# Expert weights through fifteen 8 KB buffers instead of six of 16 KB in a hybrid decoder block

## The chip, the cores and the metric

The kernel runs on one core of a Trainium2 chip. The metric is the device time of one execution in microseconds (us), read as the median of several runs; lower is better. Engine names: PE is the tensor engine (PEld its weight loads), DVE the vector engine, ACT the scalar engine, POOL the general engine, SP the engine whose queue issues most transfers. Sizes of on-chip buffers are given per partition: a buffer of 16 KB holds 16 KB in each of the 128 partitions, 2 MB in all.

## What is computed

One decoder layer on 512 tokens of width 2048, all float32:

```python
xn = rmsnorm(h, norm_mix_w)
proj = xn @ w_in                       # queries, keys, values, gates of both branches
fox_o = forgetting_attention(...)      # 8 heads
ret_o = silu(rg) * groupnorm(retention(...))   # 8 heads
merged = sum(sigmoid(gate_logit + b_gate) * (branches @ w_branch))
h = h + merged @ w_out
hn = rmsnorm(h, norm_ffn_w)
# router: best group of 4, best 2 of its 8 experts (32 experts in all)
# per token and chosen expert e:  y = (silu(x @ w1[e]) * (x @ w3[e])) @ w2[e]
h = h + weighted sum of the two y
return rmsnorm(h, norm_final_w)
```

The weights of the 32 experts are 3 x 2048 x 512 floats each, 12 MB an expert and 384 MB together. Each is read once.

## The kernel before

**First stage, up to the router.** `units_a()` lists 118 blocks of dense weights of 1 MB, two of which lie next to each other in one row of `wA`. `Stream.unit` loads two blocks at once (2 MB, a run of 16 KB in each partition) into one of two buffers of the pool `raw`, and splits each block into a rounded high part (an ACT cast, L96) and a low part (a DVE subtraction, L97) in one of two 16 KB buffers of the pool `split`. PE multiplies with these. The last dense product is `w_out` (L593 to L595); the router's logits (L557, L558) come from the same tokens and close the stage.

**Expert stage.** Every expert has one block of at most 64 tokens (`SLOTS`). `prep_e(e)` gathers them: products of a selection matrix with the three bf16 parts of the hidden state (L720, PE), gathered into `xs`. `gemm1` (matmuls at L745 named `ab<-wraw,xs`) multiplies `xs` with `w1` and `w3`, `gemm2` (matmuls at L745 named `y<-wraw,gs`) the gated result with `w2`. The result is scattered into a DRAM buffer `ybuf`. A further loop for experts with more than 64 tokens is in the program and is not entered with this data.

The weights `wM` come in pieces of 2 MB: four for `gemm1`, two for `gemm2`. A `gemm1` piece holds in each partition a run of 8 KB of `w1` and one of `w3`; a `gemm2` piece is one run of 16 KB of `w2`:

```python
loads = iter(itertools.cycle([raw, raw, split, split, raw2, raw2]))
def piece_tile(pl):
    return pl.tile([P, 2, 2048], F32, name="wraw", tag="whl" if pl is split else "wraw")
...
        for i in range(2 if part else 4):
            w = piece_tile(next(loads))
            nc.sync.dma_start(w, (w2 if part else w13)(a["wM"][e], i))
```

So six buffers go round: the two of `raw`, the two of `split`, and two of a pool `raw2` that lies in memory which the first stage uses for other things. All loads are issued on SP in the order of the program: `gemm1` of experts 0 and 1, then `gemm2` of expert e-1 behind `gemm1` of expert e+1, and so on. A load waits until PE has read what its buffer held before, and until an earlier load that used the same of eight completion semaphores has landed. The order on PE is that of a scheduler, which interleaves `gemm2`, the next gather and the next `gemm1`.

**End.** `combine` runs over four groups of 128 tokens. It reads the two expert outputs of a token from `ybuf` (2 MB a group, into the same six buffers), and per quarter of the width adds residual, outputs and the last expert's share in PSUM on PE, then `res` on DVE (L942), squares on ACT (L947), normalizes (L949 to L959) and stores. `res` lies in a buffer of `raw2`. The last expert is not scattered: its rows `ys`, and the final norm's weight `fw`, lie in the pool `yout`.

Of the kernel before, what the change touches and what calls it, by code (L numbers as in the profile page):

```python
# [21 lines left out]
P = 128  # L22
D = 2048
# [9 lines left out]
MAXBLK = 15  # L33
EPS = 1e-6
# [23 lines left out]
class Stream:  # L58


    def __init__(self, tc, raw, split):
        self.tc, self.nc, self.raw, self.split = tc, tc.nc, raw, split
        self.src, self.cur, self.half = None, None, 2

    def first(self, src):

        self.cur, self.half = self.raw.tile([P, 2, 2048], F32, name="wraw"), 0
        self.src = src

    def unit(self, src_of=None, after=None, whole=False):  # L70
        nc = self.nc
        if self.half == 2:
            self.cur, self.half = self.raw.tile([P, 2, 2048], F32, name="wraw"), 0
            nc.sync.dma_start(self.cur, src_of())
        w = self.cur[:, self.half, :]
        if whole:
            self.half += 1
            return w, None
        hl = self.split.tile([P, 2, 2048], F32R, name="whl")
        hi, lo = hl[:, 0], hl[:, 1]  # L80
        n = 2048
        if after is not None:
            with self.tc.issue_after(after[0]), self.tc.issue_after(after[1]):
                nc.scalar.copy(hi, w)
                nc.vector.tensor_sub(lo, w, hi.bitcast(F32))
            self.half += 1
            return hi, lo
        if self.src is not None:
            n = 512 if self.half == 0 else 2048
        for q in range(2048 // n):  # L90
            c = slice(q * n, (q + 1) * n)
            if self.src is not None:
                nc.sync.dma_start(w[:, c], self.src[:, self.half, c])
                if n < 2048:
                    self.fill(q)
            nc.scalar.copy(hi[:, c], w[:, c])  # L96
            nc.vector.tensor_sub(lo[:, c], w[:, c], hi[:, c].bitcast(F32))  # L97
        self.half += 1
        if self.half == 2:
            self.src = None  # L100
        return hi, lo
# [25 lines left out]
def hybrid_block(ctx, tc, a, out):  # L127
# [12 lines left out]
    raw = hold("raw", 2)  # L140
    split = hold("split", 2)
# [4 lines left out]
    def unit(kind, i, g=0, after=None):  # L146
        assert order[pos[0]] == (kind, i, g), (order[pos[0]], kind, i, g)
        k = pos[0]
        pos[0] += 1
        if k == 0:  # L150
            stream.first(a["wA"][0].rearrange("p (u n) -> p u n", u=2))
        return stream.unit(lambda: a["wA"][k // 2].rearrange("p (u n) -> p u n", u=2), after)
# [52 lines left out]
    stream.fill = lambda q: load_x(0, q)  # L205

# [13 lines left out]
    def proj_T(kind, i):  # L220
        hi, lo = unit(kind, i)
        acc = pj.tile([P, T], F32, name="acc")
        for k in range(KT):
            wh, wl = hi[:, k * P:(k + 1) * P], lo[:, k * P:(k + 1) * P]
# [5 lines left out]
    def proj_V(kind, q):  # L230
        v = [vp.tile([P, T], F32, name="v") for _ in range(NT)]
        accs = [pj.tile([P, T], F32, name="acc") for _ in range(NT)]
        for g in range(4):
            if kind == "fv" and q == 0 and g:
                load_x(g)
            hi, lo = unit(kind, q, g)
            for t in range(NT):
                for kk in range(4):
                    k = 4 * g + kk
                    s = slice(t * P, (t + 1) * P)  # L240
                    wh, wl = hi[:, kk * T:(kk + 1) * T], lo[:, kk * T:(kk + 1) * T]
# [221 lines left out]
    with pool("mtmp", 2, reuse_waits="tile") as mt:  # L463
        for j in range(KT):
            hi, lo = unit("br", j, after=done[3] if j == 1 else None)
            gs, bs = [], []
            for n in range(2):
# [4 lines left out]
                for k in range(H):  # L472
                    i = n * H + k
                    wh, wl = hi[:, i * P:(i + 1) * P], lo[:, i * P:(i + 1) * P]
# [46 lines left out]
    with pool("wr", 1, reuse_waits="tile") as wrp, pool("ht", 2, reuse_waits="tile") as ht:  # L521
# [11 lines left out]
        for c in range(4):  # L533
# [49 lines left out]
            for g in range(4):  # L583
                hi, lo = unit("wo", c, g)
                for t in range(NT):
# [3 lines left out]
                    for kk in range(4):  # L589
                        k = 4 * g + kk  # L590
                        s = slice(t * P, (t + 1) * P)
                        wh, wl = hi[:, kk * T:(kk + 1) * T], lo[:, kk * T:(kk + 1) * T]
# [35 lines left out]
    fold = rp[0].tile([P, P], F32, name="fold")  # L628
    half = P // 2
    nc.vector.tensor_add(fold[:, :half], ident[:, :half], ident[:, half:])  # L630
# [137 lines left out]
    last_ins = []  # L768
    yp = []

    def gemm2(blk, pieces, late=False):

        gs, idx = blk
        if late:
# [300 lines left out]
```

## Time and profile before

| | us |
|---|---|
| median of 3 runs (2462.07 to 2462.34) | 2462.12 |
| the profiled execution, its own time | 2461.32 |
| its span in the trace | 2459.5 |
| PE busy in the span | 2355.6 |
| DVE busy | 737.6 |
| ACT busy | 488.6 |
| POOL busy | 233.4 |

Busy time of the engines is an average over stages with different limits. The slices and the windows (rows below) tell the stages apart: in each, the unit that is never idle sets the time. A transfer is cut into packets, one for each contiguous run; 16 DMA engines share them. The profile gives the bytes and the packets of a stretch, and the share of the 16 engines' time.

### The profile page before, as it was taken

Reading aid. Unit: us, or ns where it says so; the run is one execution under the profiler, and the core shown is the slowest. Engines: PE = TensorE matmul, PEld = TensorE weight load, DVE = VectorE, ACT = ScalarE, POOL = GpSimd, SP = SyncE. Lnnn points to the kernel's source line nnn. Section 1 sums busy time; section 2 is a strip of 40 time slices with the busy share of each in tenths; the row PEclk is TensorE's granted clock in tenths of the full one; section 3 lists DMA queues with packets and bytes.
Section 4 is the critical chain, followed back from the end, with each engine's and each line's share of the span. In section 5 each row is a group of like instructions: output and inputs, shape, how many; then the busy total and the mean of one; then the engine's idle time right before and its main releaser. Section 6 shows DMA issues by size and latency. Waiting matters only on the chain. (4 is left out here: it accounts for less than half of the span.)

```text
span 2459.5 us, 35971 instructions
## 1 busy us (share of the span) xinstructions
PE 2355.6 (96%) x16110; PEld 1605.8 (65%) x16114; DVE 737.6 (30%) x1271; ACT 488.6 (20%) x617; POOL 233.4 (9%) x328
## 2 busy tenths in 40 slices
PE   8999999999999999999999979999988999999986
PEld 6888888888888888888888854544444444444422
DVE  4444445544442222244433231111111111111105
ACT  5222223222222222232223310000010000000013
POOL 0000000100100000001003121111111111111002
PEclk9999999999999999999999989999999999999998
DMA  7233334232223333244432369999999999999996
GB/s 289 98 107 128 108 101 139 79 110 73 107 78 128 128 124 117 109 151 154 146 125 87 146 267 416 414 421 422 422 421 422 422 422 422 421 422 422 422 423 249
DMA packets 85839, 594.22 MB, mean 242 GB/s; under 512 B 7800, under 2 KB 24248, under 8 KB 34640
## 3 DMA queue, kind: packets, MB, share of 16 engines
q1 hardware_dynamic: 56704, 549.48, 55.1%
q0 software_dynamic: 7856, 25.61, 3.1%
q10 hardware_dynamic: 21120, 16.78, 2.1%
q8 instruction: 128, 2.10, 0.3%
q14 instruction: 31, 0.25, 0.0%
HBM read 562.72 MB, written 37.24 MB: 244 GB/s over the span
## 5 line engine op out<-in xcount | busy, mean ns | idle before, releaser
L745 PE MATMUL ab<-wraw,xs 128*64 128x512 f32 x2048 | 461.8, 603 | 39.2 <-DMA wraw<-in_wM_dram 39.0
L225 PE MATMUL acc<-xh,whl 128*128 128x512 f32 x1152 | 453.2, 393 | 0.0
L227 PE MATMUL acc<-xh,whl 128*128 128x512 f32 x1152 | 453.2, 393 | 0.0
L226 PE MATMUL acc<-xl,whl 128*128 128x512 f32 x1152 | 452.7, 393 | 0.0
L96 ACT CAST whl<-wraw 128x2048 fp32r<-128x2048 f32 (+1 forms) x122 | 228.0, 1869 | 780.3 <-PE acc L227 412.4
L745 PEld LDWEIGHTS ab<-wraw,xs 128*64 128x64 f32 x2048 | 144.0, 138 | 325.4 <-issue 252.0
L97 DVE TENSOR_TENSOR whl<-wraw,whl 128x2048 fp32r<-128x2048 f32 (+1 forms) x122 | 275.3, 2257 | 202.2 <-ACT whl L96 201.9
L226 PEld LDWEIGHTS acc<-xl,whl 128*128 128x128 f32 x1152 | 216.4, 188 | 46.4 <-issue 1.4
L225 PEld LDWEIGHTS acc<-xh,whl 128*128 128x128 f32 x1152 | 216.5, 188 | 45.8 <-issue 0.5
L227 PEld LDWEIGHTS acc<-xh,whl 128*128 128x128 f32 x1152 | 216.4, 188 | 45.8 <-issue 1.4
L745 PE MATMUL y<-wraw,gs 128*64 128x512 f32 x1024 | 235.0, 602 | 1.7 <-DMA wraw<-in_wM_dram 1.2
L720 PEld LDWEIGHTS <-h 128*128 128x128 bf16 x6144 | 189.9, 98 | 49.5 <-issue 49.1
L720 PE MATMUL gp<-S,h 128*128 128x64 bf16 x6144 | 199.2, 193 | 1.2 <-issue 1.2
L723 DVE TENSOR_TENSOR xs<-gp,nfw 128x512 f32<-128x512 f32 x64 | 41.9, 688 | 417.0 <-PE ab L745 375.2
L745 PEld LDWEIGHTS y<-wraw,gs 128*64 128x64 f32 x1024 | 69.4, 137 | 119.2 <-issue 114.1
L705 POOL TENSOR_SCALAR S<-slot,rank 128x128 bf16<-128x128 f32 x124 | 73.4, 602 | 705.3 <-PE gp L720 673.8
L758 ACT ACTIVATE ab<-ab,rs 128x512 f32<-128x512 f32 x32 | 22.0, 687 | 524.4 <-PE ab L745 506.7
L242 PE MATMUL acc<-whl,xh 128*128 128x512 f32 x256 | 101.8, 401 | 6.2 <-ACT xh L201 6.2
L795 ACT COPY ysb<-y 64x512 f32<-64x512 f32 x62 | 35.8, 579 | 339.0 <-PE y L745 330.6
L243 PE MATMUL acc<-whl,xh 128*128 128x512 f32 x256 | 102.6, 401 | 0.0
L593 PE MATMUL acc<-whl,mh 128*128 128x512 f32 x256 | 100.4, 392 | 0.0
L594 PE MATMUL acc<-whl,mh 128*128 128x512 f32 x256 | 100.2, 391 | 0.0
(302 smaller groups left out, 2121.6 us busy)
## 6 DMA issues: line engine op xcount, KB each, us to landing
wraw<-in_wM_dram SPq DMA_DIRECT2D x192, 2048.0 KB, 23.7
wraw<-in_wA_dram SPq DMA_DIRECT2D x59, 2048.0 KB, 7.8
ybuf<-zero ACTq DMA_DIRECT2D x8, 1024.0 KB, 5.7
gate<-gs ACTq DMA_DIRECT2D x32, 256.0 KB, 2.0
g<-gate POOLq DMA_DIRECT2D x32, 256.0 KB, 2.9
wraw<-ybuf SPq DMA_DIRECT2D x4, 2048.0 KB, 26.4
xt<-in_x_dram SPq DMA_DIRECT2D x4, 1024.0 KB, 6.4
hc<-in_x_dram POOLq DMA_DIRECT2D x4, 1024.0 KB, 5.5
```

The source lines that it names most:

```text
L96: nc.scalar.copy(hi[:, c], w[:, c])
L97: nc.vector.tensor_sub(lo[:, c], w[:, c], hi[:, c].bitcast(F32))
L225: nc.tensor.matmul(acc, wh, xh[:, k], start=(k == 0), stop=False)
L226: nc.tensor.matmul(acc, wh, xl[:, k], start=False, stop=False)
L227: nc.tensor.matmul(acc, wl, xh[:, k], start=False, stop=(k == KT - 1))
L242: nc.tensor.matmul(accs[t], xh[:, k, s], wh, start=(k == 0), stop=False)
L243: nc.tensor.matmul(accs[t], xh[:, k, s], wl, start=False, stop=False)
L593: nc.tensor.matmul(accs[t], mh[k][:, s], wh, start=(k == 0), stop=False)
L594: nc.tensor.matmul(accs[t], mh[k][:, s], wl, start=False, stop=False)
L705: i = eng.tensor_scalar(S[:, t], slot1.rearrange("p a b -> p (a b)"), rsel[:, t:t + 1], None, op0=OP.is_equal)
L720: nc.tensor.matmul(gp[:, d], h3[i][:, t, (8 * g + d) * P:(8 * g + d + 1) * P], S[:, t, :SLOTS], start=(t == 0 and i == 0), stop=(t == NT - ...
L745: nc.tensor.matmul(acc[m * SLOTS:(m + 1) * SLOTS], st, w[m], start=first, stop=last)
```

## The change

The buffers are halved in size and fifteen instead of six: `raw` four of 8 KB, `split` four of 8 KB, `raw2` seven of 8 KB. The first stage loads one block of 1 MB at a time, and splits it in two halves of 1024 columns. The expert weights move in pieces of 1 MB: eight for `gemm1`, four for `gemm2`. A piece holds two runs of 4 KB in each partition, for `w2` as well. The last expert's rows `ys` and the final norm's weight `fw` move out of `yout` into the buffers `r1` and `r0` of `raw2` while the last 24 loads go round in the other thirteen. `combine` loads 1 MB at a time and writes its result over the first expert output instead of into `res`. A small matrix `fold` is no longer made.

```diff
-    raw = hold("raw", 2)
-    split = hold("split", 2)
+    raw = hold("raw", 4)
+    split = hold("split", 4)
...
+    def parts(self, w, after=None, n=1024):
...
+        for m in range(2):
+            hl = self.split.tile([P, 2, 1024], F32R, name="whl")
+            wm = w[:, m * 1024:(m + 1) * 1024]
...
+                    nc.scalar.copy(hl[:, 0, c], wm[:, c])
+                    nc.vector.tensor_sub(hl[:, 1, c], wm[:, c], hl[:, 0, c].bitcast(F32))
...
-    raw2 = scC.enter_context(pool("raw2", 2, reuse_waits="tile"))
+    raw2 = scC.enter_context(pool("raw2", 1, reuse_waits="tile"))
+    slots = [(raw, "wraw")] * 4 + [(split, "whl")] * 4 + [(raw2, f"r{i}") for i in range(NR2)]
+    loads = itertools.cycle(slots)
+    kept = set()
+
+    def buffer(shape=(P, 2, 1024), dtype=F32, name="wraw", slot=None):
+
+        if slot is not None:
+            kept.add(slots[slot][1])
+        while slot is None:
+            pl, tag = next(loads)
+            if tag not in kept:
+                break
+        else:
+            pl, tag = slots[slot]
+        return pl.tile(list(shape), dtype, name=name, tag=tag)
...
-        for g in range(4):
+        for g in range(8):
             w = next(pieces)
-            for kk in range(4):
-                k = 4 * g + kk
+            for kk in range(2):
+                k = 2 * g + kk
...
         for q in range(2):
-            w = next(pieces)
             y = psY.tile([P, DE], F32, name="y")
             for k in range(4):
-                halves_mm(y, gs[:, k], [w[:, m, k * DE:(k + 1) * DE] for m in range(2)], k == 0, k == 3)
+                if k % 2 == 0:
+                    w = next(pieces)
+                halves_mm(y, gs[:, k], [w[:, m, k % 2 * DE:(k % 2 + 1) * DE] for m in range(2)], k == 0, k == 3)
...
-        return we.rearrange("(m q) p (u n) -> m q u p n", m=3, u=2)[:2, g // 2, g % 2].rearrange("m p n -> p m n")
-
-    def w2(we, q):
-        return we[4 + q].rearrange("p (u n) -> p u n", u=2)
-
-    def pieces_of(e, part):
-        for i in range(2 if part else 4):
-            w = piece_tile(next(loads))
-            nc.sync.dma_start(w, (w2 if part else w13)(a["wM"][e], i))
+        return we.rearrange("(m q) p (u n) -> m q u p n", m=3, n=1024)[:2, g // 4, g % 4].rearrange("m p n -> p m n")
+
+    def w2(we, g):
+        return we[4 + g // 2].rearrange("p (u v n) -> v p u n", u=2, v=2)[g % 2]
+
+    def pieces_of(we, part):
+        for i in range(4 if part else 8):
+            w = buffer()
+            nc.sync.dma_start(w, (w2 if part else w13)(we, i))
             yield w
...
-            yb = piece_tile(next(loads) if first else raw)
-            nc.sync.dma_start(yb, yv[t])
-            return [[yb[:, k, c * T:(c + 1) * T] for c in range(4)] for k in range(2)]
+            ys = [buffer((P, D)) for _ in range(2)]
+            for k in range(2):
+                nc.sync.dma_start(ys[k], yv[t][:, k])
+            return ys
...
-            y0, y1 = ybs[t] if first else load_y(t)
-            r = raw2.tile([P, D], F32, name="res", tag="wraw")
+            r, y1 = ybs[t] if first else load_y(t)
...
-                nc.vector.scalar_tensor_tensor(r[:, cs], y0[c], wtf[:, 0, t:t + 1], pr,
+                nc.vector.scalar_tensor_tensor(r[:, cs], r[:, cs], wtf[:, 0, t:t + 1], pr,
                                                op0=OP.mult, op1=OP.add)
```

The change moves instructions on two engines at places that matter below. On SP, at the passage from the dense weights to the expert weights, the queue held this before (the number behind `wraw` tells tiles apart; the brackets name the semaphores that a load waits for, `DMAHW` those of SP's own earlier transfers, `DMASW` those of POOL's):

```order
L817 DMA wraw_9384<-in_wM_dram 128x2x2048 [waits DMAHW2_49,DVE_49]
L817 DMA wraw_9394<-in_wM_dram 128x2x2048 [waits DMAHW3_49,DVE_49]
L817 DMA wraw_9404<-in_wM_dram 128x2x2048 [waits PE_49]
L817 DMA wraw_9414<-in_wM_dram 128x2x2048 [waits PE_49]
L817 DMA wraw_9649<-in_wM_dram 128x2x2048 [waits DMASW4_49,DMASW5_49,DMASW3_49,DMASW6_49,DMASW2_49,Pool_49]
L817 DMA wraw_9659<-in_wM_dram 128x2x2048 [waits DMASW4_49,DMASW5_49,DMASW3_49,DMASW6_49,DMASW2_49,DMASW7_49,DMASW1_49,DMASW0_49]
L817 DMA wraw_9669<-in_wM_dram 128x2x2048 [waits DMAHW4_49,PE_49]
L817 DMA wraw_9679<-in_wM_dram 128x2x2048 [waits DMAHW5_49,PE_49]
```

Of the changed kernel the same place, from the last load into `split` on:

```order
L826 DMA wraw_9900<-in_wM_dram 128x2x1024 [waits PE_49]
L826 DMA wraw_10131<-in_wM_dram 128x2x1024 [waits DMASW3_49,DMASW2_49,DMAHW7_49,DVE_49,PE_49]
L826 DMA wraw_10137<-in_wM_dram 128x2x1024 [waits DMASW5_49,DMAHW0_49,DMASW4_49,Pool_49]
L826 DMA wraw_10143<-in_wM_dram 128x2x1024 [waits DMAHW1_49,DMASW6_49,DMASW0_49]
L826 DMA wraw_10149<-in_wM_dram 128x2x1024 [waits DMAHW2_49]
L826 DMA wraw_10155<-in_wM_dram 128x2x1024 [waits DMASW5_49,DMASW6_49,DMASW4_49,DMASW7_49,DMASW3_49,DMAHW3_49,DMASW2_49,DMASW1_49]
L826 DMA wraw_10161<-in_wM_dram 128x2x1024 [waits DMAHW4_49]
L826 DMA wraw_10167<-in_wM_dram 128x2x1024 [waits DMAHW5_49]
L826 DMA wraw_10173<-in_wM_dram 128x2x1024 [waits DMAHW6_49,PE_49]
L826 DMA wraw_10405<-in_wM_dram 128x2x1024 [waits DMAHW7_49,PE_49]
```

Eight loads of 1 MB stand ahead of `wraw_10131`, the first into `raw2` (buffer `r0`), where it was four of 2 MB; this load now waits for PE and DVE too, because `r0` lies on a pool of the router's stage (its last reader is the logits matmul, L558 of before), and it heads a queue of seven loads into `raw2`.

On PE, when `gemm1` of expert 4 (tile `ab`) and `gemm2` of expert 2 (tile `y`) run, the order before was this (gathers between left out):

```order
L745 MATMUL y_10506<-wraw_10504,gs_9993 64x512 x8
...
L745 MATMUL y_10519<-wraw_10517,gs_9993 64x512 x8
...
L745 MATMUL ab_10533<-wraw_10534,xs_10302 64x512 x8
...
L745 MATMUL ab_10533<-wraw_10544,xs_10302 64x512 x8
...
L745 MATMUL ab_10533<-wraw_10554,xs_10302 64x512 x8
```

And it is this in the changed kernel:

```order
L758 MATMUL y_11018<-wraw_11019,gs_10495 64x512 x4
L758 MATMUL y_11018<-wraw_11025,gs_10495 64x512 x4
...
L758 MATMUL ab_11051<-wraw_11052,xs_10816 64x512 x4
...
L758 MATMUL ab_11051<-wraw_11082,xs_10816 64x512 x4
...
L758 MATMUL ab_11051<-wraw_11088,xs_10816 64x512 x4
...
L758 MATMUL y_11033<-wraw_11034,gs_10495 64x512 x4
L758 MATMUL y_11033<-wraw_11040,gs_10495 64x512 x4
...
L758 MATMUL ab_11051<-wraw_11094,xs_10816 64x512 x4
```

The loads are issued in the order of their numbers. Counted from 0, `wraw_11034` and `wraw_11040` are the loads 42 and 43, and `wraw_11052` to `wraw_11094` the loads 44 to 51: the second half of this `gemm2`, which stood ahead of the next `gemm1`, now stands behind seven of its eight pieces, and its two buffers stay taken as long.

## Rows read from the trace of the kernel before

**Rows 1.** The page: mean busy share of the DMA engines, 40 slices of the span.

```profile
DMA  7233334232223333244432369999999999999996
```

**Rows 2.** Windows: start:end, length, busy of PE, PEld, DVE, ACT, POOL; clock, DMA, GB/s.

```profile
0.00:1340.00 1340.00, 1333.17 (x6080) 1097.86 (x6081) 547.02 (x819) 357.19 (x381) 84.88 (x133) 1.00 0.34 123
1500.00:1600.00 100.00, 98.83 (x1296) 52.56 (x1293) 11.98 (x28) 6.69 (x12) 12.45 (x20) 1.00 1.00 415
2300.00:2400.00 100.00, 85.22 (x568) 33.06 (x565) 9.98 (x21) 10.47 (x19) 3.60 (x4) 0.98 1.01 422
2420.00:2460.00 40.00, 21.00 (x64) 9.35 (x65) 29.06 (x77) 15.72 (x39) 10.50 (x8) 0.78 0.38 153
```

**Rows 3.** The page: issues of the expert weights' loads, and time to landing.

```profile
wraw<-in_wM_dram SPq DMA_DIRECT2D x192, 2048.0 KB, 23.7
```

**Rows 4.** DVE by line and form: the low parts of the dense weights.

```profile
L97 DVE TENSOR_TENSOR whl<-wraw,whl 128x2048 fp32r<-128x2048 f32 x118 | 272.6, 2310 | 197.2 <-ACT whl L96 196.9
L97 DVE TENSOR_TENSOR whl<-wraw,whl 128x512 fp32r<-128x512 f32 x4 | 2.8, 690 | 5.0 <-ACT whl L96 5.0
```

**Rows 5.** Timeline of SP's queue, windows of 1 us: start, duration, transfer issued.

```profile
1379.03 0.39 SPq L817 DMA_DIRECT2D wraw<-in_wM_dram  x1
...
1424.25 0.37 SPq L817 DMA_DIRECT2D wraw<-in_wM_dram  x1
...
1453.41 0.37 SPq L817 DMA_DIRECT2D wraw<-in_wM_dram  x1
...
1456.85 0.37 SPq L817 DMA_DIRECT2D wraw<-in_wM_dram  x1
```

**Rows 6.** Windows of 5 us at the passage and in the early expert stage.

```profile
1435.00:1440.00 5.00, 1.07 (x4) 0.93 (x4) 3.85 (x20) 0.09 (x1) 0.52 (x1) 0.50 0.88 365
1440.00:1445.00 5.00, 2.90 (x59) 2.82 (x60) 2.75 (x12) 0.00 (x0) 2.54 (x4) 0.50 0.00 0
...
1450.00:1455.00 5.00, 5.00 (x26) 1.66 (x24) 0.52 (x1) 0.00 (x0) 2.23 (x4) 1.00 0.17 36
1455.00:1460.00 5.00, 5.00 (x26) 1.65 (x24) 0.00 (x0) 0.00 (x0) 0.00 (x0) 1.00 0.97 400
1475.00:1480.00 5.00, 5.00 (x26) 1.72 (x24) 0.00 (x0) 0.00 (x0) 0.00 (x0) 1.00 0.92 367
1590.00:1595.00 5.00, 5.00 (x74) 2.69 (x72) 0.92 (x3) 0.58 (x1) 2.34 (x4) 1.00 0.91 359
```

**Rows 7.** Timeline of PE: last `w_out` and logits matmuls, first expert.

```profile
1422.56 0.40 PE L595 MATMUL acc<-whl,ml 128*128 128x512 f32 x1
...
1434.26 0.41 PE L558 MATMUL lg<-hl,wrs 128*100 128x256 f32 x1
...
1449.72 13.95 PE L745 MATMUL ab<-wraw,xs 128*64 128x512 f32 x64
1463.61 0.24 PE L710 MATMUL ax<-aux,S 128*128 128x40 bf16 x3
...
1469.85 13.95 PE L745 MATMUL ab<-wraw,xs 128*64 128x512 f32 x64
```

**Rows 8.** Packets of 1634:1646, in which only runs of 8 KB move.

```profile
DMA packets 658, 5.05 MB, mean 421 GB/s; under 512 B 41, under 2 KB 41, under 8 KB 41
```

**Rows 9.** Packets of 2404:2416, in which only runs of 16 KB move.

```profile
DMA packets 355, 5.14 MB, mean 429 GB/s; under 512 B 41, under 2 KB 41, under 8 KB 41
```

**Rows 10.** Packets of 2436:2438, the output's stores, in runs of 4 KB.

```profile
DMA packets 210, 0.80 MB, mean 399 GB/s; under 512 B 16, under 2 KB 16, under 8 KB 209
```

**Rows 11.** Timeline of the end: start, duration, instruction, idle before and its releaser.

```profile
2410.70 0.20 PEld L745 LDWEIGHTS y<-wraw,gs 128*64 128x64 f32 x4 [0.98 <-DMA wraw<-in_wM_dram]
...
2417.79 0.75 DVE L942 SCALAR_TENSOR_TENSOR res<-wraw,wt,ab 128x512 f32<-128x512 f32 x1
...
2435.58 0.75 DVE L942 SCALAR_TENSOR_TENSOR res<-wraw,wt,ab 128x512 f32<-128x512 f32 x1 [0.63 <-DMA out_dram<-res]
...
2437.13 1.44 PE L938 MATMUL ab<-h,idb 128*128 128x512 bf16 x3 [4.56 <-ACT ab L947]
```

More of the change, by code (lines that the diff above doesn't have):

```diff
@@ L62, in __init__ @@
         self.tc, self.nc, self.raw, self.split = tc, tc.nc, raw, split
[L63 to L101, printed above, removed]
@@ new lines, in __init__, with load @@
+        self.fill = None
+    def load(self, src):
+        w = self.raw.tile([P, 2048], F32, name="wraw")
+        self.nc.sync.dma_start(w, src)
+        return w
+    def parts(self, w, after=None, n=1024):
+        nc, res = self.nc, []
+        for m in range(2):
+            hl = self.split.tile([P, 2, 1024], F32R, name="whl")
+            wm = w[:, m * 1024:(m + 1) * 1024]
+            with ExitStack() as st:
+                for i in after or ():
+                    st.enter_context(self.tc.issue_after(i))
+                for q in range(1024 // n):
+                    c = slice(q * n, (q + 1) * n)
+                    if self.fill is not None:
+                        self.fill(2 * m + q, w)
+                    nc.scalar.copy(hl[:, 0, c], wm[:, c])
+                    nc.vector.tensor_sub(hl[:, 1, c], wm[:, c], hl[:, 0, c].bitcast(F32))
+            res.append(hl)
+        return res
@@ L149, in unit, with fill, part @@
         pos[0] += 1
-        if k == 0:
-            stream.first(a["wA"][0].rearrange("p (u n) -> p u n", u=2))
-        return stream.unit(lambda: a["wA"][k // 2].rearrange("p (u n) -> p u n", u=2), after)
+        src = a["wA"][k // 2][:, (k % 2) * 2048:(k % 2 + 1) * 2048]
+        if k:
+            hl = stream.parts(stream.load(src), after)
+        else:
+            w = raw.tile([P, 2048], F32, name="wraw")
+            def fill(q, w):
+                c = slice(q * T, (q + 1) * T)
+                nc.sync.dma_start(w[:, c], src[:, c])
+                load_x(0, q)
+            stream.fill = fill
+            hl = stream.parts(w, n=T)
+            stream.fill = None
+        def part(o, n):
+            c = slice(o % 1024, o % 1024 + n)
+            return hl[o // 1024][:, 0, c], hl[o // 1024][:, 1, c]
+        return part
     nmw = consts.tile([P, KT], F32, name="nmw")
@@ L235, in proj_V @@
                 load_x(g)
-            hi, lo = unit(kind, q, g)
+            part = unit(kind, q, g)
             for t in range(NT):
@@ L464, in hybrid_block @@
         for j in range(KT):
-            hi, lo = unit("br", j, after=done[3] if j == 1 else None)
+            part = unit("br", j, after=done[3] if j == 1 else None)
             gs, bs = [], []
@@ L769, in hybrid_block, with gemm2 @@
     yp = []
-    def gemm2(blk, pieces, late=False):
+    def gemm2(blk, pieces, ys=None):
         gs, idx = blk
+        late = ys is not None
         if late:
             wsl, sT = idx
-            ys = yp[0].tile([P, D], F32R, name="ys")
         else:
@@ L891, in hybrid_block @@
         if e == NE - 1:
-            gemm2(prev, pieces_of(e - 1, 1))
+            ys = buffer((P, D), F32R, "ys", 9)
+            gemm2(prev, pieces_of(a["wM"][e - 1], 1))
             fw = spread_fw()
-        cur = gemm1(x0, pieces_of(e, 0))
+        cur = gemm1(x0, pieces_of(a["wM"][e], 0))
         if e == 8:
@@ L993, in hybrid_block @@
             ev = nc.values_load(eid[0:1, 0:1], engines=[mybir.EngineType.SP], min_val=0, max_val=NE - 1)
[L995 to L1002 removed]
+            we = a["wM"][ds(ev, 1)].rearrange("e q p n -> (e q) p n")
+            gemm2(gemm1(prep(rsel, is2, nc.vector), pieces_of(we, 0)), pieces_of(we, 1))
         combine(diagonals())
```

43 lines of the change are left out of this document (15 added, 28 removed).

## The prediction

> **What bounds the kernel now.** I began with the page's slices, because the averages over the span mislead here: PE looks like the bound, but the DMA row stands at 2 to 4 tenths for the first 22 slices and at 9 from then to the last [rows 1]. The windows by stage say what this means [rows 2]. From 0 to 1340 us PE is busy 1333.17 us of 1340 and the DMA engines 0.34 of their time: the dense products are PE's. From 1500 on the DMA share is 1.00 to 1.01 at 415 to 422 GB/s, while PE falls to 85.22 us in 100 later on: the expert stage is bound by the stream of weights. From 2420 it is over, and the combine remains, with DVE the busiest engine and nothing full.
>
> So three things can change the time: how long the DMA engines need for what is still to be moved when the stage begins, for how long they are idle although weights are left, and what comes after the last piece. The weights' 192 loads take 23.7 us from issue to landing [rows 3], several times what 2 MB need at that rate: they queue behind each other, and latency does not count.
>
> How the stage begins is read from SP's issues and from 5 us windows. The first load was issued at 1379.03, the sixth at 1424.25, and no other until 1453.41 [rows 5]. The engines run to nearly the end of 1435 to 1440 (0.88), stand still from 1440 to 1445 and are at 0.17 of 1450 to 1455 [rows 6]: all six buffers are full, and they start again at about 1450 + 0.83 x 5 = 1454.2. What they wait for is PE's first piece. The first expert's matmuls start at 1449.72, 13.95 us for four pieces [rows 7], 3.49 us each, and SP's issues at 1453.41 and 1456.85 follow that rhythm. Later the stream has small holes only: 0.92 of 1475 to 1480 and 0.91 of 1590 to 1595 [rows 6].
>
> **What the change does, part by part.**
>
> *First stage.* Halved casts double the instructions. The subtraction takes 2310 ns for 2048 columns and 690 ns for 512 [rows 4]: 1.055 ns a column and 150 ns fixed. So 118 more of them are 118 x 150 ns = 18 us more on DVE, and about as much on ACT. DVE is busy 547 of 1340 us and ACT 357, beside a PE that is busy 1333 [rows 2]: hidden by PE, nothing. If that cover were gone it would be up to 18 us. Twice the issues cost SP some 0.4 us each [rows 5], one in 2.5 us: nothing.
>
> *Lookahead.* Fifteen buffers of 1 MB hold 15 MB where six held 12. Eight loads go out as the four did, by about 1423. The ninth, into `r0`, waits for the logits matmul, whose last ends at 1434.26 + 0.41 = 1434.7 [rows 7]; before, the sixth load went at 1424.25. I let the data flow from 1435.8. Seven loads of 2.56 us (below) then end at 1453.7. PE gives its first buffer back after a piece of 1.74 us, at 1451.5, so the stream is not interrupted. At 1453.7 it has 15 MB behind it, where before it had 12 MB and started again at 1454.2: -0.5 us, and 3 MB fewer to go. These loads fly beside the routing's short chain; were that delayed, it would cost only what goes beyond some 2 us, as long as a free buffer is there.
>
> *The rate.* What is left is 369 loads of 1 MB in runs of 4 KB, where it was 186 pieces of 2 MB: 122 in runs of 8 KB and 64 (two an expert) in runs of 16 KB. The trace has stretches with one kind alone. From 1634 to 1646, 658 - 41 = 617 runs of 8 KB go through 16 engines: 12 x 16 / 617 = 311.2 ns a run [rows 8]. From 2404 to 2416 it is 355 - 41 = 314 of 16 KB: 611.5 ns [rows 9]. Twice the bytes take less than twice the time, so a run has a fixed part: 2 x 311.2 - 611.5 = 10.9 ns. By this line a run of 4 KB takes (311.2 + 10.9) / 2 = 161 ns. No load before has 4 KB runs. The bounds: half of an 8 KB run, 155.6 ns, below, and above it the output's stores, which are 4 KB runs in the other direction, at 399 GB/s [rows 10]: 4096 x 16 / 399 = 164.3 ns. I take 160 ns, the middle of the two and close under the line, or 16 x 160 ns = 2.56 us a load. [...]
>
> Before: 122 x 16 x 0.3112 + 64 x 8 x 0.6115 = 607.5 + 313.1 = 920.6 us. After: 369 x 2.56 = 944.6 us. **+24.0 us.** At 155.6 ns it is -1.9, at 161 +30.3, at 164.3 +49.4. Other transfers (scatters, the combine's reads) stand on both sides and drop out.
>
> *New holes.* A load waits for the buffer of the load 15 before it, and SP issues in order, so a buffer that PE holds long stops all loads behind it. The order on PE, shown with the change, has that case: loads 42 and 43 are used behind loads 44 to 50. Load 57 waits for 42. PE comes to it after 51 pieces of 1.74 us and five gathers; the time from 1463.61 to 1469.85 shows one, 6.24 us [rows 7]. 1449.7 + 88.7 + 31.2 = 1569.6. The DMA engines would have finished load 56 at 1435.8 + 49 x 2.56 = 1561.2. They are idle for 8.4 us, and a us more until data flows again. An expert later the next `gemm2` is split in the same way (its second half behind seven pieces); by the same count PE is 0 to 3 us late there, and afterwards PE has caught up with the stream and waits itself. Together 11, less the holes of before (0.4 + 0.45 us in the two windows named, with others I allow 2): **+9 us**. Bounds: 0, if the gathers take less of PE than here, to 14.
>
> *The end.* The last piece lands, PE begins with it at 2410.70, and the combine's first DVE instruction follows at 2417.79 [rows 11]. The last piece is half as long: -1.7 us. In place, the combine no longer waits for the store of a `res` buffer; that wait is 0.63 us on DVE at 2435.58, and PE, which needs the PSUM that DVE frees, had been idle 4.56 us at 2437.13 [rows 11]. I take -2.3 for it, between -0.6 and -4.3. **-4 us** together. `fold` and the moves of `ys` and `fw` are off the path. 13 buffers instead of 15 for the last 24 loads matter to a stream that PE waits for only if PE holds several at a time: nothing.
>
> **Sum.** -0.5 + 24.0 + 9 - 4 = +28.5 us on the profiled execution's 2461.3, so 2489.8. The median of the runs lies 0.8 above that execution; I say **2490 us**.
>
> **Rivals.**
>
> *A: runs cost as their bytes.* Then a 4 KB run takes 155.6 ns, the rate term is -1.9, and the sum +2.6: about 2465. For it: 421 and 429 GB/s differ little. Against it: what differs goes with the run's length. [...] Chance 0.15, for 2457 to 2475; about half of it within 0.2% of before.
>
> *B, the other side: the loss at 8 KB is not one of length.* Pieces with 8 KB runs alternate between two matrices, those with 16 KB do not. If that made the 311.2 ns, and the engines otherwise move 429 GB/s at any length, a 4 KB run would take 152.8 ns, 369 loads 902 us, the term -18.7, the holes some 11 us as the stream reaches the held buffer earlier: -12, about 2450. It decides from 155.2 ns down, where the four terms are zero. Against it: the stores, at 399 GB/s, have one target. Chance 0.08.
>
> *C: the stores' rate holds for loads.* +49.4 instead of +24.0: +54, about 2515. For it: it is the only 4 KB row there is. Against it: a store goes the other way and waits on what feeds it. Chance 0.15 for above 2505.
>
> **How the numbers follow.** My forecast, 2476 to 2505, has 0.62. The range of 8 in 10 is 2464 to 2512: it leaves out B, a third of A and half of C. About 0.2%, or 5 us, is what the measurement can tell from no change. Faster: B, 0.08. Same: the half of A, 0.08. Slower: 0.84.
>
> **What the profile after would show.** The rate term: a stretch of pure weights in the later expert stage at 405 to 412 GB/s at a share of 1.0; 418 or more would be A or B, under 402 C. The lookahead: SP issues after 1424 begin at about 1434.7, and no hole from 1440 to 1450. The holes: a window at 1560 to 1572 in which the engines stand still for 8 us or so, and SP waiting there for PE's `y` matmul. The end: some 45 us from the last piece to the end of the span instead of 48.8, no wait for a store at the third group. What would make it wrong: runs of 4 KB that take under 156 ns, most of all; holes that return with every expert, if PE holds pieces behind a whole `gemm1` each time, 2 us or more each; or a first stage that grows, with PE waiting for halves of casts.

## The result and the profile after

The changed kernel takes 2523.46 us (median of 4 runs, 2522.0 to 2526.97) against 2462.23 before: a ratio of 1.025, interval 1.0232 to 1.0268. It is 61 us slower. The forecast was 28 us slower, 2490 in a range of 2464 to 2512: the sign was right, the size was not.

The profiled execution took 2524.73 us with a span of 2523.0. Of its page, the busy share of the DMA engines and the GB/s in 40 slices, and the issues of the expert weights, which answer to [rows 1] and [rows 3]:

```profile
DMA  7233333222223333443333699999999999999996
GB/s 302 87 114 124 106 130 105 92 92 101 92 96 125 125 113 118 142 150 143 132 114 101 212 394 353 381 407 392 409 409 376 407 370 409 409 363 408 376 406 237
...
wraw<-in_wM_dram SPq DMA_DIRECT2D x384, 1024.0 KB, 18.2
```

The shape is as before: a first stage on PE, then a stream of weights. But the stream is uneven. In the expert stage some slices stand at 406 to 409 GB/s, others at 353 to 394. Windows of the changed kernel (columns as in [rows 2]) say it by stage; the last two are a good and a bad stretch:

```profile
0.00:1340.00 1340.00, 1333.70 (x6084) 1098.60 (x6085) 564.15 (x933) 380.91 (x494) 79.14 (x133) 1.00 0.36 123
...
1500.00:1600.00 100.00, 98.94 (x1286) 51.56 (x1284) 11.15 (x25) 6.11 (x11) 10.03 (x15) 1.00 0.94 365
...
2100.00:2200.00 100.00, 85.06 (x850) 37.95 (x848) 10.08 (x24) 6.46 (x12) 9.92 (x15) 0.97 1.03 409
2200.00:2300.00 100.00, 93.53 (x984) 42.35 (x982) 10.33 (x25) 7.04 (x13) 9.92 (x15) 1.00 0.98 380
```

Where nothing disturbs it, the stream of 4 KB runs moves 409 GB/s, which is 4096 x 16 / 409 = 160.2 ns a run; the prediction took 160. The nine windows of 100 us from 1500 to 2400 have 365, 395, 398, 397, 399, 383, 409, 380 and 386 GB/s. Against 409 they lack 169 / 409 x 100 = 41 us; the same windows before have 415 and then 421 to 423, and lack some 2 against 422. So some 39 us more were lost to holes, where the prediction had 9.

Shorter windows of the changed kernel show where:

```profile
1430.00:1440.00 10.00, 3.94 (x24) 3.52 (x25) 7.57 (x36) 0.37 (x1) 1.45 (x3) 0.50 0.55 161
1440.00:1450.00 10.00, 9.23 (x211) 8.47 (x209) 3.05 (x10) 0.00 (x0) 3.46 (x6) 0.71 1.02 410
...
1560.00:1570.00 10.00, 10.00 (x153) 5.50 (x153) 1.45 (x3) 0.00 (x0) 0.00 (x0) 1.00 0.57 227
1570.00:1580.00 10.00, 10.00 (x82) 3.89 (x82) 2.02 (x5) 1.65 (x3) 3.31 (x5) 1.00 0.69 195
...
2220.00:2230.00 10.00, 7.97 (x107) 4.66 (x107) 3.39 (x8) 2.11 (x4) 2.15 (x4) 1.00 0.58 188
2230.00:2240.00 10.00, 10.00 (x112) 4.42 (x108) 0.16 (x1) 0.51 (x1) 1.15 (x2) 1.00 1.00 335
...
2460.00:2465.00 5.00, 5.00 (x24) 1.44 (x20) 0.00 (x0) 0.00 (x0) 0.00 (x0) 1.00 0.93 370
2465.00:2470.00 5.00, 3.14 (x16) 1.31 (x17) 1.72 (x3) 2.02 (x4) 2.98 (x5) 1.00 0.07 29
```

From 1440 to 1450 the engines now run, where they stood still before [rows 6]: the lookahead is there. The hole of 1560 to 1580 costs 4.4 + 5.2 = 9.6 us; the prediction had put it at 1561 to 1570, 8.4 us and one more. But holes like it come back, about every 165 us: at 1730 to 1750, 1890 to 1910, 2050 to 2070, 2220 to 2240 and 2380 to 2400 (2.7 to 7.2 us each, 26 together). And the stream ends at about 2465, 58 us before the end of the span, where it was 48.8 before [rows 11].

How such a hole arises is seen on PE ahead of the one at 2220. The timeline of PE in the changed kernel (start, duration, instruction, idle before and its releaser), then two transfers of SP's queue at the same time:

```profile
2195.26 3.68 PE L758 MATMUL ab<-wraw,xs 128*64 128x512 f32 x8 [5.46 <-DMA wraw<-in_wM_dram]
...
2199.63 3.87 PE L758 MATMUL y<-wraw,gs 128*64 128x512 f32 x16
2203.33 1.88 PE L758 MATMUL ab<-wraw,xs 128*64 128x512 f32 x8
...
2218.47 1.94 PE L758 MATMUL ab<-wraw,xs 128*64 128x512 f32 x8
...
2223.82 3.65 PE L758 MATMUL y<-wraw,gs 128*64 128x512 f32 x16 [0.94 <-DVE idx L752]
```

```profile
2205.32 4.68 SPq L826 DMA_DIRECT2D wraw<-in_wM_dram  x2
...
2225.79 0.37 SPq L826 DMA_DIRECT2D wraw<-in_wM_dram  x1
```

The order of the changed kernel on PE at this place, with the index of each load (counted from 0, in the order in which SP issues them) put behind it by hand:

```
L758 MATMUL ab_17260<-wraw_17261,xs_17025 64x512 x4      load 284
L758 MATMUL y_17227<-wraw_17228,gs_16704 64x512 x4       load 280
L758 MATMUL y_17227<-wraw_17234,gs_16704 64x512 x4       load 281
L758 MATMUL ab_17260<-wraw_17267,xs_17025 64x512 x4      load 285
...                                                      loads 286 to 291
L758 MATMUL y_17242<-wraw_17243,gs_16704 64x512 x4       load 282
L758 MATMUL y_17242<-wraw_17249,gs_16704 64x512 x4       load 283
```

PE first waits 5.46 us for load 284 while it already has 280 to 283. It takes that piece in 3.68 us where later ones take 1.94, does `gemm1` to load 291 with gathers between, and comes to load 282 at 2223.82. Load 297 needs that buffer, and SP issues nothing for some 16 us. The 3.68 us go with the clock: behind the 5.46 us in which PE stood idle, the window of this piece has a granted clock of 0.50, where 2205 to 2220, with the pieces of 1.94 us, has 1.00:

```profile
2195.00:2200.00 5.00, 4.74 (x22) 1.73 (x24) 0.00 (x0) 0.00 (x0) 0.00 (x0) 0.50 1.03 414
```

On this piece alone that is another 1.74 us. The loads 100, 160, 220, 280 and 340 are all passed in this way (100 by two `gemm1` pieces, the others by one). Each of these places lies ahead of one of the five later holes, and at each PE stands idle for 5.39 to 5.61 us, the piece behind that takes 3.68 us, and the granted clock is 0.50 in windows of 2 to 5 us there. The places lie 60 loads apart, the common multiple of 12 loads an expert and 15 buffers. Held halves alone make no such hole: from load 66 to load 343 the second half of every `gemm2` stands behind eight later pieces on PE, and yet most windows between the bad places have 402 to 414 GB/s. What the bad places add is that PE comes late.

The end, on all engines:

```profile
2465.28 0.69 ACT L771 ACTIVATE ab<-ab,rs 128x512 f32<-128x512 f32 x1 [11.63 <-PE ab L758]
2466.99 1.05 ACT L809 COPY ysb<-y 64x512 f32<-64x512 f32 x2
2468.34 7.09 PE L758 MATMUL y<-wraw,gs 128*64 128x512 f32 x32 [1.02 <-DVE ysb L807]
2469.38 0.94 POOL L812 DMA_INDIRECT ybuf<-ysb,idx  x1 [0.17 <-issue]
2473.47 4.53 SPq L936 DMA_DIRECT2D wraw<-ybuf  x8
2478.86 0.75 DVE L952 SCALAR_TENSOR_TENSOR wraw<-wraw,wt,ab 128x512 f32<-128x512 f32 x1
```

ACT's copy of expert 30's output stands behind its work for expert 31 (L771), so the scatter goes out at 2469.38 and the combine's reads at 2473.47, after the last weights. PE itself still has 7 us of `gemm2` to do when the stream has ended, where it waited for the last piece before [rows 11].

### The profile page after: what moved, and what is told of

Same layout as the page of the kernel before. It is cut to its first block, busy times and chain, and to the rows that moved or that the text cites. A ratio compares the mean times of both kernels' runs of the same rounds, so it can differ in the third digit from the quotient of the medians.

```text
span 2523.0 us, 36722 instructions
## 1 busy us (share of the span) xinstructions
PE 2387.2 (95%) x16114; PEld 1609.1 (64%) x16114; DVE 751.2 (30%) x1388; ACT 510.4 (20%) x735; POOL 226.7 (9%) x328
## 4 chain that ended last, share of the span: by engine, by line
PE 80%; DMA 14%; SPq 3%; DVE 1%; issue 1%; ACT 0%; POOL 0%; DVEq 0%; POOLq 0%; ACTq 0%
DMA wraw<-in_wM_dram 13%; PE ab L758 12%; PE acc L227 10%; PE acc L228 10%; PE acc L229 10%; PE y L758 6%; PE gp L733 5%; SPq L826 3%; PE acc L244 2%; PE acc L246 2%; PE acc L245 2%; PE acc L477 2%; PE acc L479 2%; PE acc L595 2%; PE acc L597 2%; PE acc L596 2%
## 5 line engine op out<-in xcount | busy, mean ns | idle before, releaser
L758 PE MATMUL ab<-wraw,xs 128*64 128x512 f32 x2048 | 487.9, 611 | 59.6 <-DMA wraw<-in_wM_dram 59.3
L84 ACT CAST whl<-wraw 128x1024 fp32r<-128x1024 f32 (+1 forms) x242 | 252.2, 1045 | 774.3 <-PE acc L229 419.1
L85 DVE TENSOR_TENSOR whl<-wraw,whl 128x1024 fp32r<-128x1024 f32 (+1 forms) x242 | 296.2, 1226 | 365.4 <-ACT whl L84 363.3
L758 PEld LDWEIGHTS ab<-wraw,xs 128*64 128x64 f32 x2048 | 137.8, 138 | 307.1 <-issue 200.1
L733 PE MATMUL gp<-S,h 128*128 128x64 bf16 x6144 | 210.0, 194 | 21.4 <-POOL S L718 16.7
L771 ACT ACTIVATE ab<-ab,rs 128x512 f32<-128x512 f32 x32 | 22.0, 687 | 634.5 <-PE ab L758 616.0
L246 PE MATMUL acc<-whl,xl 128*128 128x512 f32 x256 | 101.1, 401 | 0.0
```

What stands on the lines that cost most here:

```text
L84: nc.scalar.copy(hl[:, 0, c], wm[:, c])
L85: nc.vector.tensor_sub(hl[:, 1, c], wm[:, c], hl[:, 0, c].bitcast(F32))
L246: nc.tensor.matmul(accs[t], xl[:, k, s], wh, start=False, stop=(k == KT - 1))
L733: nc.tensor.matmul(gp[:, d], h3[i][:, t, (8 * g + d) * P:(8 * g + d + 1) * P], S[:, t, :SLOTS], start=(t == 0 and i == 0), stop=(t == NT - ...
L758: nc.tensor.matmul(acc[m * SLOTS:(m + 1) * SLOTS], st, w[m], start=first, stop=last)
```

## The experiments

Two theories stood against each other. **Held buffers:** the scheduler's order on PE no longer follows the order of the loads, so PE keeps landed pieces and waits for later ones. **The stream itself:** small pieces, eight in flight, or short runs make the holes. Each run was timed beside the kernel before (medians 2462.2 to 2463.0); the ratio is to that. The executions of one run spread over 1 to 6 us, so steps of some 4 us between two runs are uncertain by 2 to 4.

| run | us | ratio, interval |
|---|---|---|
| changed kernel | 2523.46 | 1.025, 1.0232 to 1.0268 |
| e1 PE in the order of the loads | 2488.24 | 1.0106, 1.0089 to 1.0123 |
| e2 4 KB runs in the kernel before | 2489.73 | 1.0112, 1.0095 to 1.0129 |
| e3 as e1, and the end mended | 2484.13 | 1.0088, 1.0071 to 1.0105 |
| e4 as e3, 8 KB runs | 2466.8 | 1.0013, 1.0003 to 1.0022 |
| e5 as e4, gathers between | 2453.83 | 0.9963, 0.9949 to 0.9977 |
| e6 as e3, gathers between | 2479.79 | 1.0068, 1.0051 to 1.0085 |
| e7 changed kernel, 12 buffers | 2490.48 | 1.0113, 1.0096 to 1.013 |
| e8 as e3, 12 buffers | 2488.2 | 1.0109, 1.0092 to 1.0126 |
| e9 in-place combine in the kernel before | 2458.98 | 0.9985, 0.9976 to 0.9994 |
| e10 two loads a piece in the kernel before | 2470.58 | 1.0032, 1.002 to 1.0044 |
| e11 as e5, 12 buffers | 2459.44 | 0.9987, 0.9977 to 0.9996 |
| e12 changed kernel, the end mended alone | 2518.98 | 1.023, 1.0216 to 1.0244 |

**e1, the order of use.** Each pair of the experts' matmuls is queued on PE behind the one before it in the program, which is the order of the loads.

```diff
-        for m in range(2):
-            nc.tensor.matmul(acc[m * SLOTS:(m + 1) * SLOTS], st, w[m], start=first, stop=last)
+        with ExitStack() as hs:
+            if done_mm:
+                hs.enter_context(tc.issue_after(done_mm[-1]))
+            for m in range(2):
+                i = nc.tensor.matmul(acc[m * SLOTS:(m + 1) * SLOTS], st, w[m], start=first, stop=last)
+        if chained:
+            done_mm[:] = [i.ins]
```

> The changed kernel, with one edit: PE takes the expert pieces in the order in which SP loads them (each piece's matmuls are queued behind those of the piece before). Theory of the held buffers: the holes in the weights' stream, which add up to 42 us of lost transfer time in the changed kernel, come from pieces that PE holds behind eight later ones, and from PE waiting for a later piece while it holds landed ones. They should be gone but for 3 to 8 us, the stream keeps its 409 GB/s, and the time is 2480 to 2490. The end stays late by some 8 us against before, since the last scatter still waits behind ACT's work for the last expert. Rival, the stream itself: pieces of 1 MB with at most eight in flight leave the engines idle by themselves. Then the holes stay and the time is 2515 or more.

Measured: 2488.24, 35.2 us off, within what the held buffers say. Windows of e1:

```profile
1500.00:1600.00 100.00, 93.70 (x1274) 50.24 (x1272) 11.74 (x26) 6.58 (x12) 9.93 (x15) 1.00 1.01 393
1600.00:1700.00 100.00, 97.26 (x1053) 46.38 (x1050) 14.17 (x45) 7.42 (x14) 12.27 (x19) 1.00 1.02 408
...
2200.00:2300.00 100.00, 90.14 (x1034) 42.84 (x1032) 9.97 (x25) 6.34 (x12) 9.90 (x15) 1.00 1.03 409
```

The late holes are gone at the same size of piece, the same run and the same number in flight: the stream itself does not make them. Some 4 us are still lost before 1600. The end stays as late as it was: PE begins its last `gemm2` behind DVE's copy, and the span ends 55.8 us later, at 2483.4, where the changed kernel has 54.7. So the 35 us come from the stream.

```profile
2427.58 7.09 PE L763 MATMUL y<-wraw,gs 128*64 128x512 f32 x32 [1.02 <-DVE ysb L814]
```

**e2 and e10, parts of it in the kernel before.** In e2 the `gemm1` pieces of 2 MB keep their buffers but move in runs of 1024 columns that lie 2048 apart; a piece takes two transfers. In e10 a piece takes two transfers with its old runs of 8 KB. The loads of the two, one below the other (cut; e2 also changes the view in `w13`):

```diff
+            # e2, and PE takes the same columns of xs
+            for m in range(2):
+                nc.sync.dma_start(w[:, m].rearrange("p (u n) -> p u n", u=2), s[:, m])
+            # e10
+            for m in range(2):
+                nc.sync.dma_start(w[:, m], s[:, m])
```

> The kernel before, its six buffers of 16 KB and its order of work, but the two thirds of the weights that gemm1 uses move in runs of 4 KB instead of 8 KB (a piece takes four runs of 1024 columns that lie 2048 apart, as two transfers of 1 MB; the products are the same in another order). Theory that a run of 4 KB costs 160 ns and the holes the rest: 122 pieces of 32 runs an engine at 160.2 instead of 16 at 311.2 ns, +18 us, so 2480, with no holes beyond those of before. Rival, that the run length matters little and the holes are nearly all of the loss: 2462 to 2467. Rival, that runs of 4 KB also cause the holes: 2490 or more.

> The kernel before, with each piece for gemm1 moved by two transfers of 1 MB in runs of 8 KB, into the same buffer. It is the run with 4 KB runs in the kernel before without its short runs; that one was 27 us above before, of which the rate explains 18. If the other 9 us come from two transfers a piece (eight semaphores are used up by four pieces), this run shows them: 2468 to 2474. If they come from the short runs, it stays at 2461 to 2465.

Measured: e2 2489.73, 27.4 us above its kernel before instead of 18, at the edge of the rival that short runs cause holes (2490 or more). e10 2470.58, 7.8 above, inside what two transfers were to cost. If the two costs add, 19.6 remain for the run length, against 18 expected. What the second transfer costs lies early; windows of e10, which answer to the small dips of before in [rows 6]:

```profile
1580.00:1590.00 10.00, 10.00 (x155) 5.93 (x153) 1.11 (x2) 1.07 (x2) 0.00 (x0) 1.00 0.91 357
1590.00:1600.00 10.00, 10.00 (x176) 5.92 (x172) 1.89 (x6) 1.16 (x2) 0.34 (x1) 1.00 0.71 266
```

Why two transfers in place of one open these holes was not tried further; that a piece then uses up two of eight semaphores is an argument, not shown.

**e3 and e12, the end.** For the last experts ACT's and DVE's copies of `ysb` are put ahead of the next `gemm1`'s result; e3 on top of e1, e12 in the changed kernel alone.

```diff
+            if last_y:
+                hs.enter_context(tc.issue_after(last_y[0]))
             nc.scalar.activation(sb, acc, AF.Copy, scale=rs)
...
+            if last_y:
+                hs.enter_context(tc.issue_after(last_y[1]))
             last_ins.append(nc.vector.tensor_mul(gs, tr[:, :, SLOTS:], sg))
```

> As the run with PE in the order of the loads, and for the last two experts ACT and DVE copy gemm2's result of expert 30 out of PSUM before they take up the last gemm1's result. Theory: the end of the changed kernel is late because that copy, and so the scatter and the reads of the combine behind it, stand behind ACT's work for expert 31. Then the scatter goes out some 8 us or more earlier, the reads lie beside the last weights again, and the time is 5 to 9 us below the run without this edit: 2473 to 2483. Rival, that the end is late because its reads move in smaller pieces: no change against the run without it.

> The changed kernel with the order of ACT and DVE at the end mended alone (the copies of expert 30's result before the last gemm1's). Theory: PE's order keeps PE itself late at the end, so the combine can start no sooner; only its reads are there in time: 0 to 5 us below the changed kernel, 2518 to 2524, far from the 35 us that the order of PE alone gave. If the late scatter were the main part of the late end, 10 us or more.

Measured: 4.1 us (e3 against e1) and 4.5 us (e12 against the changed kernel). The last scatters of e3 and of e12 on POOL:

```profile
2409.93 0.90 POOL L828 DMA_INDIRECT ybuf<-ysb,idx  x1 [15.60 <-DVE ysb L821]
...
2453.93 0.90 POOL L821 DMA_INDIRECT ybuf<-ysb,idx  x1 [23.81 <-DVE ysb L814]
```

In e3 it goes out at 2409.93 instead of 2428.61 (e1), in e12 at 2453.93 instead of 2469.38. So the order does delay the scatter, by 15 to 19 us, but of that only some 4 us are in the time; for e3 I had said 5 to 9. In e12 PE begins its last `gemm2` at 2465.75, only 2.6 us earlier than in the changed kernel: PE itself is late there.

**e4, runs of 8 KB.** A piece of 1 MB is 2048 columns of one matrix; PE takes two pieces at a time.

```diff
-            w = next(pieces)
-            for kk in range(2):
-                k = 2 * g + kk
+            w = [next(pieces), next(pieces)]
+            for kk in range(4):
+                k = 4 * g + kk
...
-        return we.rearrange("(m q) p (u n) -> m q u p n", m=3, n=1024)[:2, g // 4, g % 4].rearrange("m p n -> p m n")
+        return we.rearrange("(m q) p (u n) -> m q u p n", m=3, n=2048)[g % 2, g // 4, g // 2 % 2]
```

> As the run with both orders mended, and all expert pieces move in runs of 8 KB (a piece of 1 MB holds 2048 columns of w1 or of w3, or half the columns of w2; PE takes two pieces at a time and alternates between them as before). If a 4 KB run costs 160.2 ns and an 8 KB run 311.2, 369 loads take 2.490 instead of 2.563 us, -27 us: 2446 to 2456, which would be below the kernel before, by the 3 MB of lookahead and the end without the wait for a store. Pairs hold one more piece, so if buffers are short it is 2 to 5 us more. If the run length matters little, it stays where the run without this edit is.

Measured: 2466.8, a miss by some 11 us. The later stream ran at 420 GB/s, but the two windows of 100 us from 1500 to 1700 have 394 and 396: early holes of some 12 us took back part of it. Windows of e4:

```profile
1560.00:1570.00 10.00, 10.00 (x47) 3.29 (x44) 0.69 (x1) 0.58 (x1) 0.94 (x1) 1.00 0.91 338
1590.00:1600.00 10.00, 6.41 (x161) 5.08 (x159) 0.42 (x1) 0.00 (x0) 0.00 (x0) 0.96 0.60 245
1600.00:1610.00 10.00, 10.00 (x44) 3.19 (x41) 0.69 (x1) 0.58 (x1) 0.94 (x1) 0.87 0.53 182
```

and PE in e4 ahead of them, with nothing but gathers (`gp`) for 13.8 us:

```profile
1580.98 3.65 PE L763 MATMUL y<-wraw,gs 128*64 128x512 f32 x14
1584.56 5.77 PE L733 MATMUL gp<-S,h 128*128 128x64 bf16 x192
1591.89 3.91 PE L733 MATMUL gp<-S,h 128*128 128x64 bf16 x128 [1.55 <-issue]
1597.83 0.61 PE L733 MATMUL gp<-S,h 128*128 128x64 bf16 x15 [2.03 <-issue]
1598.37 5.35 PE L763 MATMUL y<-wraw,gs 128*64 128x512 f32 x16
```

**e5 and e6, gathers between.** `gemm2` is cut in two, and PE does half a gather, half of `gemm2`, the other half of the gather, the rest. The gathers' matmuls are queued in the order of the program too (left out below), so these runs pin the gathers as well as spread them. e5 has runs of 8 KB, e6 of 4 KB.

```diff
+            if g == 0 and between:
+                between()
...
+        two = gemm2_halves(prev, pieces_of(a["wM"][e - 1], 1)) if 0 < e < NE - 1 else iter([0, 0])
         if e + 1 < NE:
-            x0 = prep_e(e + 1)
-        if 0 < e < NE - 1:
-            gemm2(prev, pieces_of(a["wM"][e - 1], 1))
+            x0 = prep_e(e + 1, lambda: next(two))
+            next(two)
```

> As the run with both orders mended and runs of 8 KB, and each gather is cut in two: PE does the first half behind gemm1, then half of gemm2, then the second half of the gather, then the rest of gemm2. In the run without this edit the stream had holes of some 14 us in all before 1620 (1490 to 1500, 1560 to 1570, 1590 to 1610), where the trace shows PE at gathers for up to 14 us without giving back a piece. Theory: the gathers in a row make those holes, as all buffers are full then. They shrink to 2 to 4 us, and the time to 2453 to 2458, below the kernel before. Rival: PE holds two pieces at a time in this kernel, and this makes the holes: then 2463 or more.

> The same cut of the gathers in the run with both orders mended and runs of 4 KB (pieces used singly). Its holes before 1600 were some 5 us. Theory: they go, 2478 to 2482, against 2484 without. With the run above it shows the price of the run length without holes: 24 to 27 us between the two. If the 8 KB runs had their holes from pairs, the difference is 18 or less.

Measured: 2453.83 and 2479.79, both as the theory said. The windows of e5 that answer to those of e4, and one of its later stream:

```profile
1560.00:1570.00 10.00, 10.00 (x100) 4.58 (x100) 0.23 (x2) 0.80 (x2) 0.00 (x0) 1.00 1.02 423
1590.00:1600.00 10.00, 10.00 (x121) 5.11 (x118) 0.62 (x3) 1.07 (x2) 0.00 (x0) 1.00 1.01 421
1600.00:1610.00 10.00, 9.11 (x140) 5.21 (x137) 2.17 (x5) 0.58 (x1) 2.36 (x4) 1.00 1.01 418
...
2200.00:2300.00 100.00, 93.08 (x1004) 46.59 (x1006) 11.10 (x26) 7.76 (x14) 9.91 (x15) 1.00 1.01 420
```

Pairs alone do not make the holes. The two runs differ in the run length alone, by 26.0 us; 369 x 16 x (160.2 - 0.5 x 311.2) ns is 27. e5 is 9 us below the kernel before, the fastest of all.

**e7, e8 and e11, twelve buffers.** One number in the changed kernel, in e3 and in e5.

```diff
-NR2 = 7
+NR2 = 4
```

> The changed kernel with one number altered: four buffers in raw2 instead of seven, so twelve in all, as many bytes as before. The scheduler then gives PE another order: no piece is held behind more than six later ones (eight or nine with fifteen buffers), PE takes no gemm1 piece ahead of landed gemm2 pieces, and ACT copies the last gemm2 results in time. Theory of the held buffers and the order: the five late holes of 5 to 7 us go, the late end goes, and 3 MB of lookahead are lost, 7.7 us: 2488 to 2500, faster than with fifteen buffers. Rival, that the late holes come from too few buffers for pieces of 1 MB: with twelve they grow, 2535 or more.

> The run with both orders mended (runs of 4 KB), with twelve buffers instead of fifteen. What is left of the difference is the lookahead alone: three loads of 2.56 us that cannot land before PE gives a buffer back, less what the early holes shrink by, as the stream is less far ahead. 2488 to 2493 if the lookahead is worth 5 to 8 us; 2482 to 2486 if it is worth nothing.

> The fastest run so far (both orders mended, gathers between, runs of 8 KB) with twelve buffers instead of fifteen, the memory that the kernel before used for its six. Theory: of its 9 us below before some 5 to 7 are the lookahead of 3 MB and 2 to 3 the end. With twelve buffers 2458 to 2462. If the lookahead is worth nothing because the stream is held up by PE early on anyway, 2453 to 2456.

Measured: 2490.48, 2488.2 and 2459.44, all as expected. In the changed kernel, three buffers less make it 33 us faster, since the scheduler writes another order on PE: at the place shown above, PE takes loads 280 and 281 first, then 284 to 288, and already then 282 and 283; no `gemm1` piece goes ahead of the first half of a `gemm2`. With the order fixed, three buffers less make it 4.1 (e8 against e3) and 5.6 us (e11 against e5) slower. I put that down to the lookahead: from 1420 to 1500 e7 moves 306 GB/s and the changed kernel 346, which is 3.2 MB, three loads or some 7.7 us at 409 GB/s. Why not all of the 7.7 us are in the times of e8 and e11 was not traced.

**e9, one part alone.** The kernel before, with the combine written in place.

```diff
-            r = raw2.tile([P, D], F32, name="res", tag="wraw")
...
-                nc.vector.scalar_tensor_tensor(r[:, cs], y0[c], wtf[:, 0, t:t + 1], pr,
+                nc.vector.scalar_tensor_tensor(r[:, cs], r[:, cs], wtf[:, 0, t:t + 1], pr,
```

> The kernel before with one part of the change alone: combine writes its result over the first expert output instead of into a buffer of raw2 that an earlier store must have left. The sum of the prediction put -2.3 us on it, between -0.6 and -4.3. Theory now, from the ends of the mended runs (46.2 us from the last piece to the end, against 48.8 before, of which the half-sized last piece explains 1.7): 0.6 to 1.2 us, so 2461 to 2462. If the wait for the store had held up PE's 4.6 us as well, 2458 to 2459.

Measured: 3.8 us off, not the 0.6 to 1.2 that I expected; the other case was right. At the third group PE now waits 0.66 us where it waited 4.56 [rows 11], and DVE not at all:

```profile
2434.68 0.74 DVE L941 SCALAR_TENSOR_TENSOR wraw<-wraw,wt,y 128x512 f32<-128x512 f32 x1
2434.89 1.48 PE L937 MATMUL ab<-h,idb 128*128 128x512 bf16 x6 [0.66 <-ACT ab L946]
```

## Why the prediction was right and where it failed

**Right.** The bound: the expert stage waits for the weights' stream (2100 to 2200 has a DMA share of 1.03 beside a PE that is busy 85.06 us of 100). The *first stage*: PE is busy 1333.70 us of 1340, and DVE's 17 us more are hidden. The *rate*: 160 ns taken, 160.2 measured; +24.0 in the sum, and 26.0 between e5 and e6, which is against 8 KB throughout, while the pieces before had 16 KB runs for a third. That it came within 0.2 ns is partly luck: 160 was the middle of two bounds, one of them the rate of stores. The *first two new holes*: 9.6 us and, from 1600 to 1620, 3.1, where it said 9.4 and 0 to 3. The order and the wait are as forecast, but the close number is luck too. The engines ran dry at about 1565.5 (shares of 0.67 and 0.14 from 1564 to 1568, windows of 2 us) instead of 1561.2, and PE was late as well: it was done with load 42 at about 1571.6, where the sum should have had 1567.9. Load 57 waits for 42 alone, so 50 pieces count there and not 51.

Two more slips change nothing: the DMA row of [rows 1] also has a 7 in its first slice, a 3 and a 6 at the passage and a 6 in its last, and at 161 ns the rate term is +29.9, not +30.3.

**The step that failed** is the sentence behind the second hole, "afterwards PE has caught up with the stream and waits itself", with which the holes ended at +9. I had followed loads 42 to 69 through the order and not the loads after 100. There the order gets worse: not only do two pieces wait behind a whole `gemm1`, PE also takes one `gemm1` piece ahead of four landed `gemm2` pieces, waits for it, and is too late for the held buffers. Five more holes and smaller losses make it some 39 us where the sum had 9. These 30 us, with the 4 that e3 finds in the end, are about the 33 us that the forecast lacked. e1 shows that the order of use is the cause, e7 that it comes from the order that the scheduler writes for fifteen buffers and not from the size of the pieces. The prediction had named holes that return as what would make it wrong, and gave them no chance.

**The end** was mis-sized in both directions. Writing in place is worth 3.8 us alone, not 2.3. But expert 30's scatter goes out late, so from the end of the stream to the end of the span it is 58 us and not 45. With both orders mended it is 46.1 (in e3 PE takes its last piece at 2432.90 and the span ends at 2479.0), but the time falls by 4.1 us only, as the combine's reads then move among the last weights (issued from 2416.64 to 2433.2 in e3). It was an engine's queue that I had not followed at this place: ACT's, where the copy stands behind L771.

**The lookahead** was right in kind, with SP's issues beginning at 1433 and no standstill after 1440, and is worth 4 to 6 us by e8 and e11.

**The account by experiments:** 2523.5, less 35.2 for the order on PE (e1), less 4.1 for the end (e3), less 4.3 for the gathers (e6), less 26.0 for the run length (e5), is 2453.8. Each step is the difference of one run to the next, so this sum closes by construction. The one comparison outside it is of e11, 2459.4, which has the buffer memory of the kernel before and both orders mended, with e9, the kernel before with its combine in place, 2459.0. That they agree does not prove the parts: e11 has 8 KB runs where e9 has 16 KB for a third of the weights, some 5.6 us by [rows 8] and [rows 9], and what gives these back was not traced.

What stays open, besides: why two transfers a piece cost 8 us, whether it is the spreading or the pinning of the gathers that closes the early holes, and why the order of the scheduler turns with the number of buffers. That the 60 loads between the bad places are the common multiple of 12 and 15 is only argued.

## What to carry to other kernels

Where a ring of buffers feeds an engine, a buffer counts by how long it is held, so compare the order in which the pieces are used with the order in which they are loaded, over the whole loop and not only its first turns, after every change of their number or size (2523.46 us with fifteen buffers, 2490.48 with twelve in e7, 2488.24 with fifteen in the order of the loads in e1). If a scheduler sets the order of use, pin it to the order of the loads, and spread work that gives back no buffer between the pieces (e5, which pins that work too, is 13.0 us below e4). Halving a buffer is not free if it halves the contiguous run (26.0 us between e6 and e5): give the halves whole rows instead.

## What the runs showed of the hardware

A stream of loads of 1 MB moved 409 GB/s in runs of 4 KB and 419 to 420 in runs of 8 KB (windows of e1 and e5); loads of 2 MB in runs of 16 KB moved 429 [rows 9].

Unexpected was that the DMA engines can be busy all the time and move less. In e2 this happened with 4 KB runs behind a hole (853 of the 854 packets from 1620 to 1630 are under 8 KB):

```profile
1610.00:1620.00 10.00, 9.16 (x58) 3.41 (x55) 1.29 (x2) 0.93 (x2) 0.00 (x0) 1.00 0.99 346
1620.00:1630.00 10.00, 10.00 (x205) 6.80 (x203) 1.18 (x3) 0.72 (x2) 0.00 (x0) 1.00 1.00 331
```

At a share of 0.99 to 1.00 the rate is 331 to 346 GB/s, where the windows of 1700 to 1800 and 2200 to 2300 have 412 and 415 at 1.02. The changed kernel has it too (335 at 2230 to 2240). So the share alone does not say that a stream is at its rate. Nor is the idle time all that this hole in e2 cost: from 1600 to 1630 the shares of 0.91, 0.99 and 1.00 leave 1.0 us idle (1.9 against the 1.03 of e1's stream), and the rates of 336, 346 and 331 GB/s lack 5.2 us against 409. The cause was not tried.
